# Two transformer blocks on one core: pools held open, row-wise last products and early weight splits around the feed-forward parts

## The chip, the cores and the metric

The kernel runs on one core of one Trainium2 chip. The metric is device time of one execution in microseconds (us), lower is better.

## The reference, cut to what matters

Input `x` is 1024 rows of 1024 floats (float32). Two blocks follow one another. Each has a mixing part and a feed-forward part:

```python
# block 1
h  = rms_norm(x, norm1_g)                     # mixing: forgetting attention, a causal convolution, pooling
x  = x + mix @ w_out                          # w_out 1024 x 1024
h2 = rms_norm(x, norm2_g)
up = causal_depthwise_conv(h2 @ w_up, ffn_dw_w)   # w_up 1024 x 5632, width 3
gate, val = split(up)
x  = x + (silu(gate) * val) @ w_down          # w_down 2816 x 1024
# block 2
h  = rmsnorm(x, pre_mix_w)                    # mixing: differential and neighbourhood attention, two gates
x  = x + rmsnorm(merged @ w_out, post_mix_w)
h  = rmsnorm(x, pre_ffn_w)
f  = (silu(h @ w_gate) * (h @ w_up)) @ w_down # 1024 x 2816 twice, 2816 x 1024
x  = x + rmsnorm(f, post_ffn_w)
```

The factor of the differential attention is `exp(sum(lq1*lk1)) - exp(sum(lq2*lk2)) + 0.2`, from four vectors of 64 (the lambdas).

## The kernel before, in words

Every float32 product is made of three: an operand is split into a rounded part (`hi`, a copy on ScalarE) and a remainder (`lo`, a subtraction on VectorE or GpSimd), and `mm3` (L120) adds hi*hi, hi*lo and lo*hi. So each operand that TensorE reads has a copy and a subtraction ahead of it.

The 1024 rows are 8 blocks of 128. A program is six stages in a row: mixing 1 (`mix1`), its output product (`out1`, L690), feed-forward 1 (`ffn`, L771), mixing 2 (`mix2`, `merge2`), its output product (`out2`, L1297), feed-forward 2 (`ffn`). TensorE does nearly all of the work; the others split, add, normalise and move.

**Output products.** `proj` (L1285) multiplies one row block by 512 columns of the weights: 24 matmuls of 128x512 in all. `out1` adds the result in place to the row block in `rows[i]` and calls `done`, which is `pre_row` (L750): it stores the row to DRAM (`x1D`, on SyncE's queue), normalises it in place, and prepares the operands of the feed-forward. `out2` does the rows 0 to 3 (`second`, L1312) with three `o` buffers, then the columns of rows 4 to 7, opens the pools of the next stage (`early`, L1342), and only then transposes rows 0 to 3. Both are inside `mixing()` (L106), which holds the pools `hT` (the transposed operand, 64 KB a partition), `w` (weights) and `ps` (PSUM: tags tr 2, mm 2, sc 3, pv 1).

**The way up** (`ffn_up`, L789) takes the first product by Strassen's rule in Winograd's form: seven products of half size per channel of 128 columns, with seven transposed operands `T1` to `T7`. `T1` and `T2` are transposed in `pre_row` (`put`, L740); the sums for `T3` to `T7` are formed there (L765 to L768) and transposed after the mixing's pools are closed (`puts`, L902), between the products of channels 0 and 1. A channel's weights come by `weights_a` (L804: two loads of 512 KB and one split) and `weights_b` (L814: sums and three splits); for channels 0 and 1 the loads go out on ScalarE's queue (L897). `lo_of` (L783) sends the subtractions to GpSimd and VectorE in turn, by a counter. There are 22 channels; the result goes to DRAM (`gD`).

**The way down** (`ffn_down`, L966) is a Strassen product again, in groups of 2, 3, 3 and 3 pairs. `load` (L983) brings operands, each is split (L1027 to L1033), and for each of the seven products `DOWN` (L41) four row blocks get 6 or 9 matmuls. `to` (L1003) adds the result to `acc`. In the last group product 7, 4, 3 and 2 follow one another, each for four blocks; `done` (L1044) is called on rows 4 to 7 during product 4 and on rows 0 to 3 during product 2. After the first feed-forward `done` is `stored` (L1381: store to `x2D`, norm in place), after the second it is `final2` (L1411: load `x3D`, norm, add, store). Mixing 2 begins with the transposes of the rows (`to_T`, L170); `lam` (L1065) is called there (L1186).

The order of instructions on each engine is not the program's: the Tile framework orders them by a simulated timeline, with the program's order as priority. Queues run what they got in order. Pools are stacks: one opened after another was closed lies in its memory and waits, tile by tile, for the last use there.

## Time and profile before

| | us |
|---|---|
| median of 3 runs (lowest to highest) | 2841.91 (2841.21 to 2844.3) |
| the profiled execution, its own time | 2845.55 |
| its span, first to last instruction | 2843.8 |
| TensorE busy / VectorE / ScalarE / GpSimd | 2687.9 / 1798.9 / 1200.4 / 891.6 |
| mean granted TensorE clock, as a share of 2.4 GHz | 0.980 |

All durations below come from the one profiled execution. A view by stretches gives the busy time of each engine in a stretch, with the number of instructions behind "x", and the mean granted clock; idle time is the length less the busy time. In a timeline the number in brackets is the idle time of the engine just before the instruction, and what ended it.

### The profile page before, as it was taken

Reading aid. Unit: us, or ns where it says so; the run is one execution under the profiler, and the core shown is the slowest. Engines: PE = TensorE matmul, PEld = TensorE weight load, DVE = VectorE, ACT = ScalarE, POOL = GpSimd, SP = SyncE. Lnnn points to the kernel's source line nnn. Section 1 sums busy time; section 2 is a strip of 40 time slices with the busy share of each in tenths; the row PEclk is TensorE's granted clock in tenths of the full one; section 3 lists DMA queues with packets and bytes.
Section 4 is the critical chain, followed back from the end, with each engine's and each line's share of the span. In section 5 each row is a group of like instructions: output and inputs, shape, how many; then the busy total and the mean of one; then the engine's idle time right before and its main releaser. Section 6 shows DMA issues by size and latency. Waiting matters only on the chain.

```text
span 2843.8 us, 37039 instructions
## 1 busy us (share of the span) xinstructions
PE 2687.9 (95%) x13686; PEld 2258.3 (79%) x13686; DVE 1798.9 (63%) x2748; ACT 1200.4 (42%) x1879; POOL 891.6 (31%) x626
## 2 busy tenths in 40 slices
PE   8999889899999999999999999998997999999997
PEld 7799767678888778788888978887776788887786
DVE  4697574668878799736766443443427555555977
ACT  4344562344544543425545344444323333334333
POOL 3256322123333134611112254422423111211345
PEclk9999999999999999999999999999998999999999
DMA  5445342223332563265554495415412233335722
GB/s 182 122 124 146 115 158 97 82 78 100 107 111 97 207 244 122 93 194 139 155 162 128 126 209 140 133 62 180 157 77 78 82 102 106 111 101 191 260 89 93
DMA packets 317678, 374.01 MB, mean 132 GB/s; under 512 B 42613, under 2 KB 215089, under 8 KB 316985
## 3 DMA queue, kind: packets, MB, share of 16 engines
q1 hardware_dynamic: 309176, 367.45, 41.9%
q10 hardware_dynamic: 8320, 4.19, 0.5%
q8 instruction: 108, 1.77, 0.3%
q14 instruction: 74, 0.60, 0.1%
HBM read 256.49 MB, written 115.08 MB: 131 GB/s over the span
## 4 chain that ended last, share of the span: by engine, by line
PE 69%; DVE 10%; DMA 10%; issue 4%; POOL 3%; ACT 2%; SPq 1%; DVEq 0%; POOLq 0%; ACTq 0%
PE x L118 21%; PE mm L118 20%; PE y L118 11%; PE sc L118 5%; PE z L118 4%; PE pv L118 4%; DVE ac L550 2%; PE tr L359 2%; DVE x L1000 1%; DMA x<-in_w_down_dram 1%; PE tr L1105 1%; DMA x<-gD 1%; DMA mixD<-pvt 1%; DMA wr<-in_w_out_dram 1%; DVE r L1010 1%
## 5 line engine op out<-in xcount | busy, mean ns | idle before, releaser
L139 POOL TENSOR_TENSOR wl<-wr,wh 128x1024 fp32r<-128x1024 f32 x71 | 179.8, 2536 | 359.2 <-ACT wh L138 300.6
L787 POOL TENSOR_TENSOR hl<-x,hl 128x1024 fp32r<-128x1024 f32 x63 | 172.3, 2750 | 278.7 <-ACT hl L1031 197.9
L1031 ACT CAST hl<-x 128x1024 fp32r<-128x1024 f32 x154 | 153.2, 1050 | 221.9 <-PE x L118 123.5
L317 ACT ACTIVATE t<-t,mx 128x640 f32<-128x640 f32 (+3 forms) x192 | 172.9, 901 | 164.6 <-DVE mx L313 156.9
L118 PE MATMUL x<-hl,hl 128*128 128x512 f32 x704 | 214.1, 391 | 3.6 <-DVE hl L787 3.6
L787 POOL TENSOR_TENSOR w<-ws,w 128x1024 fp32r<-128x1024 f32 x44 | 135.4, 3078 | 250.7 <-ACT w L800 250.7
L787 POOL TENSOR_TENSOR w<-wr,w 128x1024 fp32r<-128x1024 f32 (+1 forms) x44 | 85.7, 1947 | 397.7 <-ACT w L800 397.7
L118 PE MATMUL mm<-hA,wh 128*128 128x512 f32 x608 | 197.6, 399 | 4.7 <-ACT gs L1231 4.7
L118 PE MATMUL mm<-hB,wh 128*128 128x512 f32 x608 | 196.7, 397 | 1.0 <-ACT gs L1231 1.0
L365 DVE TENSOR_TENSOR pl<-tr,ph 128x512 fp32r<-128x512 f32 (+2 forms) x160 | 100.5, 634 | 120.0 <-DMA yD<-pvt 42.6
L334 POOL TENSOR_SCALAR t<-t,rs 128x640 f32<-128x640 f32 (+7 forms) x128 | 107.4, 846 | 201.9 <-DVE rs L333 159.8
L877 DVE SCALAR_TENSOR_TENSOR r<-r,fdw,r 128x1024 f32<-128x1024 f32 x88 | 122.2, 1406 | 72.2 <-ACT r L875 72.1
L118 PE MATMUL y<-hl,hl 128*128 128x512 f32 x528 | 161.0, 390 | 5.7 <-DVE hl L787 5.7
L118 PE MATMUL mm<-wh,hB 128*128 128x256 f32 (+1 forms) x752 | 162.2, 305 | 3.0 <-ACT hB L180 3.0
L800 ACT CAST w<-wr 128x1024 fp32r<-128x1024 f32 (+1 forms) x88 | 73.6, 838 | 216.2 <-PE x L118 126.0
L118 PEld LDWEIGHTS x<-hl,hl 128*128 128x128 f32 x704 | 132.8, 189 | 32.3 <-DVE hl L787 4.8
L118 PE MATMUL mm<-wh,hA 128*128 128x256 f32 (+1 forms) x704 | 150.6, 301 | 6.3 <-ACT hA L180 2.1
L787 DVE TENSOR_TENSOR hl<-x,hl 128x1024 fp32r<-128x1024 f32 x91 | 140.7, 1553 | 8.7 <-ACT hl L1031 8.4
L118 PE MATMUL x<-hl 128*128 128x512 f32 x352 | 134.2, 393 | 4.9 <-DVE r L1010 4.7
L118 PEld LDWEIGHTS mm<-hA,wh 128*128 128x128 f32 x608 | 115.5, 192 | 29.2 <-ACT gs L1231 5.3
L843 ACT COPY r<-x 128x512 f32<-128x512 f32 x132 | 76.7, 581 | 145.4 <-PE x L118 87.1
L364 ACT CAST ph<-tr 128x512 fp32r<-128x512 f32 (+2 forms) x160 | 85.2, 542 | 123.7 <-PE tr L359 85.9
(350 smaller groups left out, 7720.5 us busy)
## 6 DMA issues: line engine op xcount, KB each, us to landing
gD<-r SPq DMA_DIRECT2D x154, 256.0 KB
x<-gD SPq DMA_DIRECT2D x154, 256.0 KB
wr<-in_w_up_dram SPq DMA_DIRECT2D x60, 512.0 KB
wr<-in_w_in_dram SPq DMA_DIRECT2D x50, 512.0 KB
x<-in_w_down_dram SPq DMA_DIRECT2D x88, 256.0 KB
wr<-in_w_gate_dram SPq DMA_DIRECT2D x20, 512.0 KB
wr<-in_w_out_dram SPq DMA_DIRECT2D x16, 512.0 KB
QS<-q2D SPq DMA_DIRECT2D x32, 256.0 KB
```

The lines of the kernel that those rows point to most:

```text
L118: self.nc.tensor.matmul(out, lhsT, rhs, start=start, stop=stop, **kw)
L139: g = (lo_engine or nc.gpsimd).tensor_tensor(out=lo, in0=raw[:, :n], in1=hi.bitcast(F32), op=ALU.subtract)
L317: nc.scalar.activation(out=t[:, :nb * P], in_=t[:, :nb * P], func=AF.Exp, scale=-1.0, bias=m, accum_out=s)
L334: nc.gpsimd.tensor_scalar(out=t[:, :nb * P], in0=t[:, :nb * P], scalar1=r, scalar2=1.0, op0=ALU.mult, op1=ALU.mult)
L359: nc.tensor.transpose(tr[:, o * P:(o + 1) * P], ts[qb][:, c:c + P], self.ident)
L364: nc.scalar.copy(out=ph[:, :w], in_=tr[:, :w])
L365: nc.vector.tensor_tensor(out=pl[:, :w], in0=tr[:, :w], in1=ph[:, :w].bitcast(F32), op=ALU.subtract)
L787: return eng.tensor_tensor(out=lo, in0=raw, in1=hi.bitcast(F32), op=ALU.subtract)
L800: nc.scalar.copy(out=hi, in_=raw)
L843: nc.scalar.copy(out=snaps[j], in_=pts[c]["x"])
L877: nc.vector.scalar_tensor_tensor(out=t, in0=src[:, 2 - s:2 - s + S], scalar=self.fdw[:, 2 - s, cc:cc + 1], in1=t, op0=ALU.mult, op1=ALU.add)
L1031: nc.scalar.copy(out=hi, in_=raw)
```

## The change

The pools `hT` and `ps` stay open through the way up: `T4` to `T7` lie in the buffers of the transposed operand, and the way up uses the mixing's PSUM tags. `T5` and `T6` are transposed row by row in `pre_row`; the first weight is loaded and split during the output product (`w_early`). The sums `out1` and `out2` write go to buffers `o` (two in `out1`, one in `out2`), from which rows are stored and normalised; `out2` takes the rows one after another. The first weight loads move from ScalarE's to SyncE's queue (`w_load` issues with `nc.sync`). In the way down, the first splits have a higher priority, the last two products are taken row by row, and the norm's steps by halves; `stored` normalises rows 0 to 3 into other buffers. `lam` is called in mixing 1.

```diff
-        with self.pool("hT", 2) as self.hpool, self.pool("w", 3) as self.wpool, self.pool("ps", 2, PSUM) as self.ps_mix:
+        stack = ExitStack()
+        self.hpool = stack.enter_context(self.pool("hT", 1))
+        self.ps_mix = stack.enter_context(self.pool("ps", 2, PSUM))
+        self.close_mixing = stack.close
+        with self.pool("w", 3) as self.wpool:
             yield
...
+        with self.pool("pe") as pe:
+            gB = self.bcast_row(I["norm2_g"][0], pe)
+            self.w_early(pe.tile([P, D], F32, tag="o", name=self.n("o"), bufs=2))
+            for i in range(NB):
+                o = pe.tile([P, D], F32, tag="o", name=self.n("o"), bufs=2)
+                part(i, 0, w0, o)
+                part(i, 1, w1[6:] if i < 4 else w1, o)
+                done(i, gB, o)
...
-    def pre_row(self, i, rows, keep, gB, jk, T, pool, ps):
+    def pre_row(self, i, rows, gB, src, T, pool, ps):
...
-        self.norm_rows(x, x, jk, gB)
+        self.norm_rows(src, x, x, gB)
...
+        if i == 4:
+            T[6], T[5] = self.T_in("hA", 0), self.T_in("hB", 0)
...
-        self.sums[j] = {6: t2, 5: b11, 7: k0, 4: b21, 3: k1}
+        self.put(T, 6, j, t2, ps)
+        self.put(T, 5, j, b11, ps)
+        self.sums[j] = {7: k0, 4: b21, 3: k1}
...
+    def w_early(self, raw):
+        raw = self.w_load(0, 0, raw.rearrange("p (h x) -> p h x", h=2))
+        self.w_split(0, (1, 2), raw.rearrange("p h x -> p (h x)"), self.nc.vector)
+
+    def w_split(self, c, which, raw, eng=None):
+        w = 512 * len(which)
+        hi, lo = ((self.early_hl.pop().tile([P, 1024], F32R, tag="w", name=self.n("w")) if self.early_hl else
+                   self.fw.tile([P, 1024], F32R, tag="w", name=self.n("w"), bufs=8))[:, :w] for _ in range(2))
+        self.nc.scalar.copy(out=hi, in_=raw)
+        if eng is None:
+            self.lo_of(lo, raw, hi)
+        else:
+            eng.tensor_tensor(out=lo, in0=raw, in1=hi.bitcast(F32), op=ALU.subtract)
...
-            pts[c] = {n: ps.tile([P, 512], F32, tag=n, name=self.n(n)) for n in ("y", "x", "z")}
+            pts[c] = {n: ps.tile([P, 512], F32, tag=t, name=self.n(n), bufs=b)
+                      for n, t, b in (("y", "sc", 3), ("x", "mm", 2), ("z", *(("sc", 3) if c % 2 else ("pv", 1))))}
...
-            weights_a(c, nc.scalar)
+            weights_a(c, nc.vector)
+        T[7], T[4] = self.T_in("hA", 1), self.T_in("hB", 1)
+        T[3] = tuple(fT.tile([P, 4, 512], F32R, tag=f"T3{x}", name=self.n(f"T3{x}")) for x in "hl")
...
+        for c in (0, 1):
+            begin(c)
+            product(c, 1, "x", True)
+            product(c, 2, "z", True)
+            if c == 0:
+                weights_b(0, second=False, eng=nc.vector)
+        snap(0, 1)
+        puts(7)
+        product(0, 6, "x", False)
+        snap(0, 2)
+        product(0, 5, "y", True)
         puts(4)
+        weights_b(0, first=False)
         g11(0)
...
         p7(0)
         v22(0)
+        puts(3)
+        close_sums()
         p4(0)
+        weights_b(1)
         product(1, 6, "x", False)
...
+            def whole(r, h):
+                mss[r, h] = self.sm(1, f"fm{h}", 8)
+                nc.scalar.activation(out=junk[:, :512], in_=acc[r][:, h * 512:(h + 1) * 512], func=AF.Square,
+                                     accum_out=mss[r, h])
+                if h == 0:
+                    nc.gpsimd.tensor_tensor(out=mss[r, 0], in0=mss[r, 0], in1=mss[r, 1], op=ALU.add)
+                    done(r, self.rsqrt(mss[r, 0], 1.0 / D), acc, spare)
...
+            for i in DOWN[:5] if last else DOWN:
+                if gi == 0 and i in (1, 5):
+                    with self.tc.high_priority(offset=100):
+                        hl = operands(i)
+                else:
+                    hl = operands(i)
...
+            if last:
+                h3, h2 = operands(3), operands(2)
+                y2 = [ps.tile([P, 512], F32, tag="b", name=self.n("y")) for _ in range(4)]
+                for i, b in ((3, 0), (3, 1), (2, 0), (3, 2), (2, 1), (3, 3), (2, 2), (2, 3)):
+                    block(i, b, *((h3, y[b]) if i == 3 else (h2, y2[b])))
...
-            with self.pool("lam") as pl:
-                self.lam(pl)
...
-        for i in range(NB):
-            nc.sync.dma_start(out=rows[i][:, :D], in_=xD[i * P:(i + 1) * P, :])
-        with self.pool("pq", 1) as pq:
+        with self.pool("p5", 4) as pp, self.pool("pq", 1) as pq:
+            w0 = []
+            for k in (0, 2, 4, 6):
+                raw = pq.tile([P, D], F32, tag="o" if k % 4 else "gf", name=self.n("o"))
+                w0 += self.pair_in(W, k, 0, raw, [(pp, "woh", 4), (pp, "wol", 4)])
+            for i in range(NB):
+                nc.sync.dma_start(out=rows[i][:, :D], in_=xD[i * P:(i + 1) * P, :])
...
+            half = [first(i) for i in range(4)]
+            for i in range(NB):
+                pts = (self.proj(i, mT, w0), half[i] if i < 4 else first(i))
+                o = pq.tile([P, D], F32, tag="o", name=self.n("o"))
...
+                nc.vector.tensor_tensor(out=o, in0=o, in1=rows[i][:, :D], op=ALU.add)
+                nc.sync.dma_start(out=yD[i * P:(i + 1) * P, :], in_=o)
+                done(i, gB, o)
...
+        o = spare(True) if i < 4 else acc[i]
+        nc.vector.scalar_tensor_tensor(out=o, in0=acc[i], scalar=r, in1=held["g"], op0=ALU.mult, op1=ALU.mult)
```

`pair_in` is a load with a split whose subtraction is VectorE's; `T_in` takes a buffer of the pool `hT` as the pair of one `T`. The last norm (`final2`) does its multiplication, addition and store for the two halves of a row in turn, with all eight rows of `x3D` loaded when the last group begins.

## Rows read from the trace of the kernel before

**Rows 1.** The page, busy time of the engines

```profile
PE 2687.9 (95%) x13686; PEld 2258.3 (79%) x13686; DVE 1798.9 (63%) x2748; ACT 1200.4 (42%) x1879; POOL 891.6 (31%) x626
```

**Rows 2.** Busy time by stretch: from:to, length, PE, PEld, DVE, ACT, POOL, PEclk, DMA, GB/s

```profile
640.00:940.00 300.00, 300.00 (x1310) 244.62 (x1309) 243.09 (x253) 143.86 (x172) 98.38 (x31) 1.00 0.32 103
...
500.00:600.00 100.00, 87.24 (x389) 69.29 (x388) 64.54 (x83) 38.00 (x55) 19.97 (x14) 0.93 0.23 67
955.00:1075.00 120.00, 105.33 (x438) 82.77 (x437) 106.83 (x116) 52.77 (x63) 27.04 (x11) 0.97 0.72 256
1185.00:1230.00 45.00, 38.94 (x243) 35.24 (x242) 31.32 (x36) 21.80 (x34) 23.53 (x19) 0.92 0.52 172
2040.00:2095.00 55.00, 47.94 (x190) 37.77 (x189) 12.42 (x12) 12.72 (x22) 19.72 (x16) 0.91 0.41 152
2130.00:2230.00 100.00, 82.19 (x365) 64.76 (x365) 64.04 (x84) 38.99 (x64) 27.22 (x23) 0.90 0.22 68
2585.00:2695.00 110.00, 101.73 (x434) 81.78 (x433) 89.26 (x102) 45.09 (x57) 24.35 (x10) 0.98 0.74 262
```

**Rows 3.** Prices: chain of waits at 1088.96 (start, us, what); timeline of PE at 2125.99

```profile
1088.96 8.16 PE x L118 x36
...
2125.99 1.04 PE L744 MATMUL tr<-ident,r 128*128 128x128 f32 x8
```

**Rows 4.** Busy time by stretch, transposes of L744 alone (PE, PEld, clock, DMA)

```profile
500.00:600.00 100.00, 12.71 (x84) 10.46 (x84) 0.93 0.23 67
...
2130.00:2230.00 100.00, 16.32 (x96) 12.84 (x96) 0.90 0.22 68
```

**Rows 5.** Timeline of PE at the start of both ways up, the longest stalls

```profile
524.40 0.70 PE L118 MATMUL x<-T1h,w 128*128 128x512 f32 x1 [3.70 <-ACT w L800]
...
543.17 1.16 PE L744 MATMUL tr<-ident,r 128*128 128x128 f32 x8 [2.02 <-DVE T6l L748]
...
2161.71 0.73 PE L118 MATMUL x<-T1h,w 128*128 128x512 f32 x2 [2.14 <-POOL w L787]
```

**Rows 6.** Timelines of VectorE and the chain of waits in the first output product

```profile
518.21 1.28 DVE L188 SCALAR_TENSOR_TENSOR r<-r,rr,wr 128x1024 f32<-128x1024 f32 x1 [3.10 <-DMA x1D<-r]
...
513.93 4.15 DMA x1D<-r
```

**Rows 7.** Timelines of SyncE's and ScalarE's queues and ScalarE at the second way up

```profile
2088.76 68.70 SPq L1326 DMA_DIRECT2D x3D<-r  x8
...
2145.30 0.37 ACTq L808 DMA_DIRECT2D wr<-in_w_gate_dram  x1
...
2154.03 1.04 ACT L800 CAST w<-wr 128x1024 fp32r<-128x1024 f32 x1 [3.63 <-DMA wr<-in_w_gate_dram]
```

**Rows 8.** Timelines of ScalarE and VectorE, a row of the second output product

```profile
2084.15 0.60 ACT L1318 ACTIVATE o<-mm 128x512 f32<-128x512 f32 x1 [6.86 <-PE mm L118]
...
2087.51 1.23 DVE L1325 TENSOR_TENSOR r<-o,r 128x1024 f32<-128x1024 f32 x1
```

**Rows 9.** Timelines of PE and SyncE's queue, from merge2 to out2

```profile
2053.17 0.50 PE L118 MATMUL sc<-wl,hA 128*128 128x512 f32 x1 [2.19 <-POOL wl L139]
...
2070.28 0.83 PE L118 MATMUL mm<-woh,hA 128*128 128x512 f32 x2 [3.65 <-ACT woh L138]
...
2057.64 15.42 SPq L135 DMA_DIRECT2D wr<-in_w_out_dram  x3
```

**Rows 10.** Timeline of VectorE at the end of the first way down

```profile
1205.85 4.32 DVE L188 SCALAR_TENSOR_TENSOR r<-r,rr,x 128x1024 f32<-128x1024 f32 x2 [0.90 <-DMA x2D<-r]
```

**Rows 11.** Timeline of PE at the start of the first way down

```profile
981.37 0.79 PE L118 MATMUL x<-hl,hl 128*128 128x512 f32 x2 [2.12 <-DVE hl L787]
```

**Rows 12.** The end: timeline of PE, and busy time by stretch

```profile
2826.14 0.61 PE L118 MATMUL y<-hl,hl 128*128 128x512 f32 x2
...
2800.00:2827.00 27.00, 26.76 (x119) 21.82 (x117) 23.31 (x23) 10.80 (x15) 15.45 (x11) 1.00 0.22 82
2827.00:2840.00 13.00, 0.00 (x0) 0.00 (x0) 11.02 (x11) 3.95 (x8) 7.84 (x8) 0.69 0.66 245
```

More of the change, by code (lines that the diff above doesn't have):

```diff
@@ L41 @@
 DOWN = (1, 5, 6, 7, 4, 3, 2)
-LATE = (6, 5, 7, 4, 3)
+LATE = (7, 4, 3)
 NX = 26
@@ L717, in out1 @@
             part(i, 1, w1[:6])
-        gB, jk = (self.wpool.tile([P, D], F32, tag="wr", name=self.n("wr"), bufs=2) for _ in range(2))
-        nc.sync.dma_start(out=gB, in_=I["norm2_g"][0].partition_broadcast(P))
-        for i in range(NB):
-            part(i, 0, w0)
-            part(i, 1, w1[6:] if i < 4 else w1)
-            done(i, gB, jk)
+        with self.pool("pe") as pe:
[6 more added lines that the diff above has]
+                done(i, gB, o)
     def right_rows(self, name):
@@ L1029, in ffn_down @@
                     raw = loaded[p][i].rearrange("p a b -> p (a b)")
-                    hi, lo = (fh.tile([P, 1024], F32R, tag="hl", name=self.n("hl"), bufs=12) for _ in range(2))
+                    if last and i == 2:
+                        hi, lo = (fx.tile([P, 1024], F32R, tag="x", name=self.n("hl"), bufs=NX) for _ in range(2))
+                    else:
+                        hi, lo = (fh.tile([P, 1024], F32R, tag="hl", name=self.n("hl"), bufs=12) for _ in range(2))
                     nc.scalar.copy(out=hi, in_=raw)
```

280 lines of the change are left out of this document (128 added, 152 removed).

## The prediction

> **What bounds the kernel.** The page comes first: TensorE is busy 95% of the span, no other engine over 63% [rows 1]. So the next view is busy time by stretch. Inside the first way up TensorE is busy 300.00 of 300 us at full clock [rows 2]; the second looks the same. What TensorE loses, it loses at the seams between stages, and the change touches seams only. For each I count the matmuls and give them the price of an undisturbed run: 8.16 us for 36 matmuls of 128x512 is 0.227 us each, 1.04 us for 8 transposes is 0.13 us each [rows 3]. Length less that sum is the loss, idle time and slow clock together.
>
> - First way up, 500 to 600: 389 instructions, 84 of them transposes [rows 2, 4]. 305 x 0.227 + 84 x 0.13 = 80.1, loss 19.9.
> - Second way up, 2130 to 2230: 269 and 96 [rows 2, 4]: 73.5, loss 26.5.
> - First way down, 955 to 1075: 438 [rows 2]: 99.3, loss 20.7.
> - Second way down, 2585 to 2695: 434 [rows 2]: 98.4, loss 11.6.
> - merge2 to out2, 2040 to 2095: 190 [rows 2]: 43.1, loss 11.9.
> - First way down to mixing 2, 1185 to 1230: matmuls of two lengths, so I take idle time alone, 45 - 38.94 = 6.1 [rows 2]; with the clock of 0.92 it is up to 9.
> - The end: the last matmul ends at 2826.75 [rows 12], the span at 2843.8: 17.
>
> Together some 115 us lie open. Next, timelines at each seam say what ended the stalls.
>
> **The change, part by part.**
>
> *First way up: gain 15.* TensorE waited 3.70 us for the first weight's copy and then stood before transposes whose buffers waited for a subtraction, 2.02 us [rows 5]; the clock was 0.93 in the mean [rows 2]. Afterwards channel 0's first weight is split during `out1`, T5 and T6 of rows 4 to 6 are transposed there, and four products (48 matmuls, 10.9 us) can run as soon as row 7's projection is over. Beside them row 7 takes its chain: add, square, power, scaling, four subtractions, two puts, about 9 us by VectorE's steps (0.6 to 1.3 each, as in [rows 6, 8]). So most of the loss goes; I leave 5 us for channel 1's weights and for T7. Bounds 6 to 18: all of it save the last chain, or only the first wait and its clock.
>
> *Second way up: gain 15.* The same, from a larger loss: TensorE stood 2.14 us for GpSimd's subtraction of a weight [rows 5], and rows 4 to 7 came every 5.45 us (24 matmuls), together with the puts of rows 0 to 3. Now rows 4 to 7 come every 10.9 us. But the new loads of channels 0 and 1 lie in the memory of the weights that row 7 still reads. Before, the third of such loads took from 2145.30 plus about 1 us to 2154.03 [rows 7], nearly 8 us; then copy and subtraction, 2.3. The first two products cover 5.4 us, so I leave a stall of 5, its slow clock and some 6 more. Bounds 5 to 22.
>
> Here the queue matters too. The loads were ScalarE's; now they stand in SyncE's queue among the stores of rows, each of which waits for its row: eight issues spread over 68.70 us, the last at about 2157, while ScalarE's load went out at 2145.30 [rows 7]. A load put behind the last store is up to 12 us late; I count 4 of that in the 11 left. The Trainium skill, "DMA: Bandwidth & Descriptors", section "Issuing engines are not separate DMA queues", says that all issuing engines feed the same 16 DMA engines, so that another issuer saves only the sequencer's time, "usually small relative to the DMA itself". By that sentence the move costs nothing, and the sum would gain 4 more; the row of 68.70 us shows a queue that waits, which the page doesn't speak of.
>
> *Row buffers: cost 6.* In `out1` norms waited for a store to land (3.10 us, the store itself 4.15) because the row was normalised in place [rows 6]; that goes. In its place a buffer `o` is held from the first addition until the store lands, 2.7 + 4.15 = 6.9 us. With two, rows can come every 3.4 us, and rows 0 to 3 want 2.7 (12 matmuls): about 2 us lost. In `out2` there is one `o`: from the square to the end of the addition 2084.15 to 2088.74 [rows 8], plus a store of 4.15: 8.7 us a row, against 5.45 us for rows 0 to 3 and 10.9 for 4 to 7. Two PSUM buffers and the projections that can go ahead cover the most; I take 4. Bounds 0 to 20 (four rows of each product late by the difference and the clock down).
>
> *merge2 to out2: gain 8.* TensorE stood 3.65 us for the weights of the second half, since their loads were queued behind eight row loads (SyncE's queue, 15.42 us for three) [rows 9]. Now these weights load first, four projections instead of three cover them, and the rows follow. The wait of 2.19 us for the first half's last subtraction [rows 9] stays. Bounds 3 to 10.
>
> *First way down to mixing 2: gain 3.* VectorE's norm waited for the store of the row (0.90 us) and ran at twice its cost beside GpSimd (4.32 us for two) [rows 10]. Rows finish one by one now, and out of place. But the buffers of the last operand lie where the low part of the transposed rows goes, so these subtractions wait for the last matmul. Bounds -2 to 6.
>
> *Starts of the ways down: gain 6 of 32.* A subtraction was late by 2.12 us [rows 11], and priority brings that forward; the PSUM of the first blocks comes free earlier. The later stalls there stand beside a VectorE busy 106.83 of 120 us and DMA at 0.72 [rows 2], which the change leaves. Bounds -2 to 15.
>
> *The end: gain 2.* After the last matmul VectorE is busy 11.02 of 13 us, and before that 23.31 of 27 [rows 12]: it is the bound, and its work stays (halves cost a little more). What goes is its idle time and half of the last store. Bounds -4 to 8.
>
> *Lambdas: 0.* Four small loads, a few steps of VectorE and an exponential go from a seam into mixing 1; TensorE covers them there. Bounds -1 to 1.
>
> *The loops: cost 2.* The splits that now name VectorE don't advance the counter of `lo_of`. From channel 2 on, the first way up has each split's subtraction on the other engine: VectorE gets two of 1024 columns (1.2 us each) for one of 1024 and one of 512. It was busy 243.09 of 300 us [rows 2], about 15.6 a channel, and gets 0.6 more. Bounds 0 to 20 (1 us in each of 20 channels).
>
> Sum: 15 + 15 - 6 + 8 + 3 + 6 + 2 + 0 - 2 = 41. The profiled execution took 2845.55 us, 3.64 over the median of the runs; against it 2804.6, against the median 2801.
>
> **The rivals.**
>
> *All seams close.* The upper bounds together (18 + 22 + 10 + 6 + 15 + 8 + 1 = 80) give 2762. For it: VectorE and GpSimd are far from full in the way up's seams (64 of 100 us) [rows 2]. Against: row 7's chain and the loads remain. Chance 0.1.
>
> *The stalls move.* The ways up start late all the same, because channel 0's and 1's loads wait in SyncE's queue or for memory, and the seams of the ways down don't change: 6 + 5 - 6 + 8 + 3 + 2 + 2 - 2 = 18, so 2824. For it: the queue row [rows 7]. Against: the first split no longer hangs on it. Chance 0.2. That priorities change no order (the scheduler may place the splits as before) is in this case.
>
> *Slower: the flipped subtractions.* In the first way up the late split goes to GpSimd beside a VectorE that has the convolution. If a product then waits in each channel, and the clock falls with it, 20 channels pay. It decides from 41 / 20 = 2 us a channel on; at 2.6 us it is 52, a net loss of 11, so 2853. For it: VectorE's 81%. Against: not one wait of TensorE in 300 us [rows 2]. Chance 0.07.
>
> *No change within the bound*, gains and costs cancelling: 0.05.
>
> **How the numbers follow.** Forecast 0.58, with a range of its own from 2781 to 2818; the rivals as above. 2801 is the likeliest. The range of 2780 to 2832 takes in the forecast, the case of moved stalls and a little of the better case. A measurement of this kernel can tell about 0.2% (5.7 us) from no change. Faster by more: 0.58 + 0.1 + 0.2 = 0.88, less 0.01 for the slow edge of moved stalls: 0.87; same 0.05; slower 0.08.
>
> **What would show it.** In the changed profile: the stretch between the last projection and the first full channel has no weight wait over 2 us in the first way up, and one of about 5 in the second; out2's first weight wait is 2 us; idle time at mixing 2's start is some 3 us; the end after the last matmul takes 13 to 16 us; TensorE stays at 300 of 300 in the loops. Wrong if channels lengthen over 19.3 us, if the rows of `out2` are paced by `o`, or if the second way up still loses over 20.

## The result, and the profile after

The changed kernel takes **2809.05 us** (median of four runs, 2807.82 to 2809.56); the kernel before, run beside it, 2841.56 (2839.91 to 2844.3). The ratio is **0.9882, 95% interval 0.987 to 0.9895**: 32.5 us less, where 41 were forecast. The profiled span is 2807.2 us against 2843.8, 36.6 less, and the mean granted clock 0.985 against 0.980.

The page has no other engine near the bound (it answers to [rows 1]):

```profile
PE 2675.4 (95%) x13686; PEld 2253.3 (80%) x13686; DVE 1811.5 (65%) x2772; ACT 1207.4 (43%) x1913; POOL 821.6 (29%) x634
```

TensorE still has 13686 instructions and is busy 12.5 us less: it stands less, and less of its time has a low clock. Where, is read from the starts and ends of the stages in TensorE's timelines of both kernels (us; "way up" begins behind the last matmul of the output product, "way down" at its first matmul):

| stretch | before | after | difference | the prediction's terms for it |
|---|---|---|---|---|
| mixing 1 and first output product | 519.8 | 519.3 | -0.5 | lambdas 0, `o` +2 |
| first way up | 458.2 | 446.3 | -11.9 | -15, loops +2 |
| first way down | 225.2 | 225.8 | +0.7 | starts of both, -6 |
| mixing 2, to the end of merge2 | 845.5 | 848.2 | +2.7 | -3 |
| second output product | 96.5 | 86.3 | -10.3 | -8, `o` +4 |
| second way up | 465.2 | 449.3 | -15.8 | -15 |
| second way down | 216.3 | 218.2 | +1.9 | (above) |
| after the last matmul | 17.05 | 13.7 | -3.4 | -2 |

So four stretches gained about what was forecast or more, the ways down gained nothing, and mixing 2 lost. The next view, busy time by stretch of the changed kernel, answers to [rows 2, 12]; its columns are from:to, length, PE, PEld, DVE, ACT, POOL, PEclk, DMA, GB/s.

```profile
519.20:600.00 80.80, 70.59 (x312) 56.96 (x311) 54.19 (x65) 36.70 (x51) 13.28 (x8) 0.92 0.21 63
600.00:900.00 300.00, 300.00 (x1313) 246.19 (x1312) 244.00 (x250) 143.73 (x171) 59.04 (x32) 1.00 0.33 105
...
965.00:1085.00 120.00, 107.66 (x455) 85.94 (x456) 114.59 (x121) 51.12 (x60) 36.50 (x13) 0.99 0.74 258
1185.00:1205.00 20.00, 15.46 (x87) 13.18 (x86) 12.20 (x15) 9.37 (x18) 8.65 (x12) 0.91 0.62 214
...
1935.00:1950.00 15.00, 13.83 (x47) 10.46 (x48) 5.86 (x9) 5.32 (x9) 3.71 (x3) 0.77 0.66 198
1950.00:1965.00 15.00, 11.89 (x48) 8.76 (x47) 6.46 (x7) 4.81 (x6) 9.99 (x5) 0.95 0.50 154
2040.00:2130.00 90.00, 89.31 (x417) 73.75 (x416) 51.85 (x60) 30.36 (x65) 18.12 (x39) 1.00 0.20 73
2126.00:2206.00 80.00, 68.39 (x308) 53.57 (x308) 49.93 (x67) 32.65 (x50) 16.96 (x11) 0.96 0.27 83
2575.00:2685.00 110.00, 103.38 (x446) 83.27 (x447) 105.97 (x113) 48.66 (x58) 35.52 (x13) 1.00 0.72 256
...
2793.50:2807.20 13.70, 0.01 (x1) 0.00 (x0) 9.72 (x16) 1.45 (x4) 5.21 (x7) 0.60 0.41 154
```

Three things are to be seen. The loops lose nothing (300.00 of 300), and the second output product is full (89.31 of 90). At the start of the first way down VectorE is busy 114.59 of 120 us: a full engine. And a new hole stands at 1935 to 1965, at the start of merge2, with a clock of 0.77. Both kernels wait 3.45 us for the first gate at this place; behind that the kernel before has no wait over 1.35 us, the changed one has 2.80 for a weight's copy and 2.46 for VectorE.

The longest stalls of TensorE in the ways up, from its timeline (they answer to [rows 5]; in brackets the idle time before, and what ended it):

```profile
527.27 1.09 PE L760 MATMUL tr<-ident,t 128*128 128x128 f32 x4 [4.31 <-DVE t L782]
...
574.50 3.01 PE L123 MATMUL y<-hB,w 128*128 128x512 f32 x12 [1.36 <-DVE r L886]
581.82 5.49 PE L123 MATMUL x<-hA,w 128*128 128x512 f32 x12 [4.30 <-ACT r L893]
...
2135.23 0.50 PE L123 MATMUL x<-T1h,w 128*128 128x512 f32 x1 [2.89 <-ACT w L816]
...
2145.51 1.09 PE L760 MATMUL tr<-ident,t 128*128 128x128 f32 x4 [3.83 <-DVE t L782]
```

No wait for a weight is left in the first way up, and one of 2.89 us in the second; the chain of row 7 (`t`, L782) is what TensorE waits for now, and a copy on ScalarE (L893) that the prediction didn't have. In the second way up that chain isn't new: before, TensorE stood 3.45 us for it, longer than the 2.14 us of [rows 5]. And in the first, channel 1's weight stands just beside it: ScalarE's copy of that weight waited for its load and ended at 526.15, 1.1 us before TensorE goes on (TensorE before, then ScalarE of the changed kernel):

```profile
2149.14 0.97 PE L744 MATMUL tr<-ident,t 128*128 128x128 f32 x4 [3.45 <-DVE t L766]
```

```profile
525.11 1.04 ACT L816 CAST w<-wr 128x1024 fp32r<-128x1024 f32 x1 [1.48 <-DMA wr<-in_w_up_dram]
```

Where in the ways up the gain lies, the prediction's own count tells (a matmul 0.227 us, a transpose 0.13; in the first 100 us of each way up the kernel before has 80 transposes, the changed one 64). These are the first 100 and the last 80 us of both, the kernel before, then the changed one:

```profile
519.80:619.80 100.00, 87.97 (x392) 70.00 (x390) 68.80 (x84) 44.38 (x61) 24.45 (x11) 0.93 0.24 74
898.00:978.05 80.05, 76.51 (x326) 61.32 (x324) 57.54 (x60) 36.67 (x45) 17.81 (x6) 0.98 0.41 136
2145.25:2245.25 100.00, 82.19 (x356) 64.60 (x355) 64.27 (x82) 37.68 (x56) 24.74 (x14) 0.90 0.27 82
2530.40:2610.40 80.00, 76.92 (x328) 62.44 (x328) 33.95 (x38) 25.17 (x34) 12.38 (x7) 0.98 0.39 130
```

```profile
519.30:619.30 100.00, 89.80 (x396) 72.72 (x395) 69.66 (x82) 44.81 (x60) 17.01 (x10) 0.93 0.25 77
885.60:965.65 80.05, 78.60 (x343) 63.98 (x342) 61.02 (x64) 38.40 (x47) 12.62 (x7) 1.00 0.36 115
2126.00:2226.00 100.00, 88.39 (x395) 69.96 (x395) 61.27 (x80) 40.10 (x59) 20.66 (x13) 0.97 0.29 90
2495.30:2575.30 80.00, 78.37 (x342) 63.78 (x340) 37.63 (x44) 26.12 (x36) 12.37 (x7) 1.00 0.34 115
```

The loss at the start fell from 18.8 to 16.3 us in the first way up and from 27.0 to 16.5 in the second; at the end it fell from 6.1 to 2.2 and from 5.5 to 2.4. The rest is work that now runs ahead, in the output products: 16 transposes of each way up (2.1 us), and 12 matmuls of channel 0's product with `T2` in the first (2.7 us), of which this is a part:

```profile
503.68 0.63 PE L123 MATMUL z<-T2h,w 128*128 128x512 f32 x2
```

### The profile page after: what moved, and what is told of

The parts are those of the page before. It is cut to its first block, busy times and chain, and to the rows that moved or that the text cites. A ratio compares the mean times of both kernels' runs of the same rounds, so it can differ in the third digit from the quotient of the medians.

```text
span 2807.2 us, 37120 instructions
## 1 busy us (share of the span) xinstructions
PE 2675.4 (95%) x13686; PEld 2253.3 (80%) x13686; DVE 1811.5 (65%) x2772; ACT 1207.4 (43%) x1913; POOL 821.6 (29%) x634
## 4 chain that ended last, share of the span: by engine, by line
PE 74%; DMA 9%; DVE 9%; issue 3%; ACT 2%; POOL 2%; SPq 1%; DVEq 0%; POOLq 0%; ACTq 0%
PE mm L123 23%; PE x L123 21%; PE y L123 12%; PE sc L123 5%; PE z L123 4%; PE pv L123 4%; PE tr L371 2%; DMA x<-in_w_down_dram 2%; DVE ac L563 1%; DVE x L1047 1%; DMA mixD<-pvt 1%; PE tr L1184 1%; DVE r L1057 1%; DVE hl L841 1%; PE tr L760 1%
## 5 line engine op out<-in xcount | busy, mean ns | idle before, releaser
L123 PE MATMUL x<-hA,w 128*128 128x512 f32 x1056 | 257.0, 394 | 4.5 <-ACT r L893 4.3
L123 PE MATMUL mm<-hA,wh 128*128 128x512 f32 x608 | 242.9, 399 | 3.5 <-ACT gs L1308 3.5
L123 PE MATMUL mm<-hA,wl 128*128 128x512 f32 x608 | 240.1, 395 | 0.0
L123 PEld LDWEIGHTS x<-hA,w 128*128 128x128 f32 x1056 | 199.8, 190 | 47.8 <-ACT r L893 5.5
L123 PE MATMUL mm<-wh,hA 128*128 128x256 f32 (+1 forms) x704 | 211.7, 301 | 3.4 <-ACT hA L192 2.8
L123 PE MATMUL mm<-wl,hA 128*128 128x256 f32 (+1 forms) x704 | 210.4, 299 | 0.9 <-DVE wl L144 0.9
L123 PE MATMUL mm<-wh,hB 128*128 128x256 f32 (+1 forms) x704 | 209.7, 298 | 0.2 <-DVE hB L193 0.2
L841 POOL TENSOR_TENSOR w<-wr,w 128x512 fp32r<-128x512 f32 x42 | 54.8, 1304 | 460.1 <-ACT w L816 460.1
L841 DVE TENSOR_TENSOR w<-wr,w 128x1024 fp32r<-128x1024 f32 (+1 forms) x42 | 52.0, 1238 | 179.1 <-ACT w L816 173.7
L816 ACT CAST w<-wr 128x512 fp32r<-128x512 f32 (+1 forms) x86 | 71.6, 833 | 208.5 <-PE x L123 116.5
L927 DVE SCALAR_TENSOR_TENSOR r<-r,fdw,r 128x1024 f32<-128x1024 f32 x88 | 140.0, 1610 | 16.9 <-ACT r L925 16.8
```

Of the source, the lines that this page charges most:

```text
L123: self.nc.tensor.matmul(out, lhsT, rhs, start=start, stop=stop, **kw)
L816: self.nc.scalar.copy(out=hi, in_=raw)
L841: return eng.tensor_tensor(out=lo, in0=raw, in1=hi.bitcast(F32), op=ALU.subtract)
L927: nc.vector.scalar_tensor_tensor(out=t, in0=src[:, 2 - s:2 - s + S], scalar=self.fdw[:, 2 - s, cc:cc + 1], in1=t, op0=ALU.mult, op1=ALU.add)
```

## The experiments

Each stands beside runs of the kernel before on the same chip, so that ratios are compared: the change has 0.9882 (0.987 to 0.9895). An interval is some 4 us wide to either side; smaller effects are read from the stretches of the profiled executions. These have a spread of their own: the changed kernel and those of experiments 1, 2, 3, 5, 6, 7 and 10 wait at the same places of the first way up's start, 10.2 us in all, and yet it takes 443.6 to 443.9 us in five of them (mean granted clock of its first 120 us 0.97) and 445.8 to 446.3 in three, the changed one among them (0.94). There a difference under 2.7 us says nothing.

**1. Row loads of the second output product.** In SyncE's queue of the changed kernel, at merge2's start:

```profile
1909.62 0.43 SPq L1393 DMA_DIRECT2D r<-x2D  x1
...
1912.77 8.62 SPq L1393 DMA_DIRECT2D r<-x2D  x7
```

In the kernel before they went out 140 us later, just ahead of the product that reads them:

```profile
2050.84 3.80 SPq L1302 DMA_DIRECT2D r<-x2D  x8
```

The edit keeps them behind merge2's gate loads:

```diff
-                    nc.sync.dma_start(out=g, in_=self.gD[8 * j + m])
+                    self.mark = nc.sync.dma_start(out=g, in_=self.gD[8 * j + m])
...
-                nc.sync.dma_start(out=rows[i][:, :D], in_=xD[i * P:(i + 1) * P, :])
+                d = nc.sync.dma_start(out=rows[i][:, :D], in_=xD[i * P:(i + 1) * P, :])
+                self.tc.add_manual_dep(d.ins, self.mark.ins.name, NOSYNC, reason="late")
```

> The changed kernel, with the eight loads of x2D rows for the second output product ordered behind the last gate load of merge2 (order alone, no wait added). Theory: merge2 begins 8.5 us late in the changed kernel because these 4 MB now go out at 1909.62 to 1921, ahead of the loads of yD and of the first branch weights (the copy of wh waits 2.80 us, TensorE's clock is 0.77 between 1935 and 1950). Then the stretch from the last matmul of the first way down to the last of merge2 shrinks from 848.2 us by 5 to 9, no weight wait over 1.5 us is left at merge2's start, and the rows land before the second output product needs them, so that this one stays at 86.3: some 2802 in all. Rival: the late start of merge2 comes from its own loads and the stores of the gates in the queue, as in the kernel before; then the stretch shrinks by less than 2 us. A second way to lose: the rows now stand in front of the weights of the second output product as before, which gives back 5 us or more there.

Ratio 0.9837 (0.9823 to 0.985), median 2797.89: faster than the change, the intervals don't touch; the span is 2798.8 us, 8.4 less. The stretch from the first way down to the end of merge2 is 842.4 us (848.2), the output product 86.26. SyncE's queue and the busy time by stretch of this kernel:

```profile
2007.97 1.39 SPq L1393 DMA_DIRECT2D r<-x2D  x3
2012.21 3.66 SPq L1393 DMA_DIRECT2D r<-x2D  x5
```

```profile
1930.00:1945.00 15.00, 13.45 (x58) 10.47 (x57) 5.27 (x8) 6.72 (x11) 3.79 (x2) 1.00 0.66 215
2033.00:2123.00 90.00, 89.31 (x417) 73.77 (x416) 51.45 (x59) 30.82 (x65) 17.60 (x38) 1.00 0.20 71
```

The clock of the stretch is 1.00 instead of 0.77, no weight wait is left there, and the second output product doesn't wait for the rows. The theory holds. Of the 8.4 us, 5.8 stand in this stretch. By the count of TensorE's instructions in mixing 2 the changed kernel is 18.0 us ahead of the kernel before at the 4000th and 9.9 at the 4400th; this one is ahead by 15.2 and 16.2.

**2. The lambdas.** The edit moves the call of `lam` from mixing 1 (L475) back to mixing 2, in a pool with two buffers.

> The changed kernel with the lambdas computed in mixing 2, as in the kernel before, and not in mixing 1. Theory: in mixing 1 they cost 3 us (between instructions 100 and 550 TensorE falls behind the kernel before by 3.1 us, the four loads go out at 48.47 to 49.81 and VectorE waits 3.39 us for them). Then instruction 550 comes 3 us earlier and mixing 2 gets at most 3.5 us longer. Since mixing 1's end stalls on other things, the first output product's end may come 0 to 3 us earlier than 519.3. In all 2806 to 2812. Rival: the 3 us are another order of the same instructions, not the lambdas; then instruction 550 stays where it is, within 0.5 us, and the total too.

Ratio 0.9899 (0.9885 to 0.9913): not faster. TensorE's instruction 550 comes at 93.3 us (94.7 in the change, 93.0 before, so that the change is 1.7 us late there, not 3.1), and by instruction 800 this kernel is behind the change by 0.2. Mixing 1 ends at 519.0. So the theory falls: at instruction 550 the lambdas had 1.4 us, which didn't last. In mixing 2 the stretch got 4.6 us longer, and the trace shows the lambdas there: their loads stopped VectorE 4.34 us ahead of the way down's last addition, and TensorE stood 5.56 us where the change has 0.79 (VectorE, then TensorE):

```profile
1191.98 0.29 DVE L1147 TENSOR_TENSOR lp<-lt 128x128 f32<-128x128 f32 x1 [4.34 <-DMA lt<-in_lambda_k_dram]
```

```profile
1193.68 1.54 PE L189 MATMUL tr<-ident,r 128*128 128x128 f32 x6 [5.56 <-DVE neglam L1153]
```

In the kernel before they ran at 1218.6, and nothing waited for them. So it is the place in the order that costs, not the lambdas.

**3. First splits on both engines.**

```diff
-                    self.lo_of(lo, raw, hi, 2 if gi else 1)
+                    self.lo_of(lo, raw, hi)
```

> The changed kernel, where the first group of both ways down sends every second low subtraction to GpSimd (now all are VectorE's there). Theory: the starts of the ways down gained nothing, because the stalls there (0.8 to 2.1 us each, nine in 120 us) wait for a VectorE that is busy 114.59 of 120 us; the order, which the higher priority changed, isn't what they wait for. Then taking some 14 subtractions of 1.2 us off VectorE lowers its busy time there by 10 to 15 us of 120, and TensorE's busy time in the first 120 us of the first way down rises from 107.66 by 3 to 8: the two ways down get 3 to 12 us shorter together, 2800 to 2806. Rival: VectorE and GpSimd slow each other down (a subtraction of VectorE was seen at 2.4 to 3.4 us instead of 1.2 beside GpSimd), or the stalls are those of loads (DMA share 0.74): then the ways down change by less than 2 us or get longer.

Ratio 0.9959 (0.9946 to 0.9972): 22 us slower than the change by the spans (2829.7), the rival's side by far. The ways down take 235.1 and 222.6 us (225.8 and 218.2), 13.6 us more together; 7.5 stand in mixing 2, where nothing was edited. The timelines of GpSimd, VectorE and TensorE show why:

```profile
967.68 2.38 POOL L841 TENSOR_TENSOR hl<-x,hl 128x1024 fp32r<-128x1024 f32 x1 [15.66 <-ACT hl L1094]
978.24 12.28 POOL L841 TENSOR_TENSOR hl<-x,hl 128x1024 fp32r<-128x1024 f32 x1 [8.16 <-ACT hl L1094]
```

```profile
967.73 2.89 DVE L1047 TENSOR_TENSOR x<-x,x 128x512 f32<-128x512 f32 x1
```

```profile
990.57 3.58 PE L123 MATMUL y<-hl,hl 128*128 128x512 f32 x8 [6.41 <-POOL hl L841]
```

The two engines hold each other up, whichever began first. GpSimd's first subtraction took 2.38 us, and VectorE's of a loaded operand (L1047), begun 0.05 us behind it, took 2.89, where others of its kind took 0.69. GpSimd's second began while VectorE ran one step behind another, and took 12.28 us. The mean of VectorE's subtractions of L1047 rose from 997 to 1235 ns:

```profile
L1047 DVE TENSOR_TENSOR x<-x,x 128x512 f32<-128x512 f32 x36 | 44.1, 1235 | 4.4 <-DMA x<-in_w_down_dram 4.1
```

VectorE's busy time fell only to 107.03 us in 120, and TensorE waited 6.41 us for GpSimd. So VectorE is full there, but handing every second of these subtractions to GpSimd makes it worse. The Trainium skill, "SBUF — State Buffer", section "Who interferes with whom", says that VectorE and GpSimd share a port pair by an exclusive lock, and that a VectorE instruction with two inputs in SBUF contends with GpSimd's reads; these rows agree.

**4. The early split of channel 0's first weight.** Both calls of `w_early` are taken out.

> The changed kernel without the early load and split of channel 0's first weight in both output products: it is loaded and split at the start of the way up, on SyncE's queue like channel 1's. Theory: the early split carries most of the gain of the two ways up (11.9 and 15.9 us), since the first two products can only start on it. Then the first matmul of the first way up comes 4 to 9 us after the last of the output product, that of the second 6 to 14 us, and the sum is 10 to 20 us over 2809: 2819 to 2829. Rival: the gain comes from the pools that stay open, so that the loads find free memory early and T5 and T6 are ready; then the loads hide in the rows' chain and the loss is under 4 us for both.

Ratio 0.9875 (0.9859 to 0.9891), 2808.08 us: no slower than the change. The first matmuls come 3.57 and 4.94 us late, but the ways up as a whole take 448.3 and 450.7 us, only 1.9 and 1.4 more, and mixing 1 with its output product 2.9 less. Most of the 2.9 us are the 12 matmuls of channel 0's product with `T2`, which now run in the way up again. While TensorE waits for the weight, VectorE finishes row 7's chain: the wait of 4.31 us at 527.27 isn't there in this kernel. Two waits stood side by side, and the change removed one. The theory falls.

**5. Where the last operand lies.** `operands(2)` of the last group takes tiles of the ring `hl` instead of the loads' ring `x` (L1090 to L1093 become one line).

> The changed kernel, where the operand of the last product of both ways down lies in the ring of the other split operands, and not in the loads' ring, whose memory the low part of mixing 2's transposed rows takes over. Theory: at mixing 2's start TensorE waits for these low subtractions (1.58 and 1.62 us), which can't run before the last matmul has read that operand; so the first matmul of mixing 2 comes 4 to 5.5 us after the last of the way down, not 6.7. The price: the operand's splits must wait for the last matmul of product 4 (the ring has 12 tiles), which may stop TensorE for 0 to 2 us before product 2 at both ends. Between -3 and +2 in all. Rival: the weights decide, whose loads SyncE's queue lets go only at 1192.64, after the stores of rows; then the first matmul of mixing 2 stays 6 to 7 us behind, and only the cost of the ring is seen.

Ratio 0.9902 (0.9887 to 0.9916). The first matmul of mixing 2 comes 7.7 us after the last of the way down (6.75 in the change), and TensorE still waits 1.19 and 1.17 us for the same low subtractions. So the memory of that operand is some 0.4 us of each of these waits (1.58 and 1.62 in the change). The end after the last matmul grew to 16.9 us (below).

**6. The stores of rows on another queue.**

```diff
-        nc.sync.dma_start(out=x2D[i * P:(i + 1) * P, :], in_=acc[i])
+        nc.scalar.dma_start(out=x2D[i * P:(i + 1) * P, :], in_=acc[i])
```

> The changed kernel, with the eight stores of x2D at the end of the first way down issued on ScalarE's queue instead of SyncE's. Theory of the queue: these stores hold SyncE's queue for 20.30 us until 1192.64, and mixing 2's first weights wait behind them; on the other queue the weights go out before 1189 and are split before the last matmul, and the first matmul of mixing 2 comes 1 to 3 us earlier than 6.7 us after the last of the way down. Rival: the low part of the transposed rows decides, which lies in the memory of the last operand: then it comes at 6 to 7 us all the same, or later, since ScalarE's copies now stand behind stores that wait for their row.

Ratio 0.989 (0.9874 to 0.9907). The weights went out 17 us earlier, but their copy ran only at 1200.08, behind ScalarE's squares and copies of the last rows (SyncE's queue, then ScalarE):

```profile
1175.90 1.67 SPq L140 DMA_DIRECT2D wr<-in_w_in_dram  x2
```

```profile
1200.08 1.05 ACT L143 CAST wh<-wr 128x1024 fp32r<-128x1024 f32 x1
```

Mixing 2's first matmul came 9.8 us after the way down's last, later than in the change. Neither of the two causes that I had for this seam is enough by itself. In the changed kernel two chains end side by side. One is that of the last row, in VectorE's timeline:

```profile
1191.51 0.69 DVE L1057 TENSOR_TENSOR r<-y,r 128x512 f32<-128x512 f32 x1 [0.55 <-PE y L123]
1192.99 1.28 DVE L1451 SCALAR_TENSOR_TENSOR x<-r,rr,x 128x1024 f32<-128x1024 f32 x1 [0.79 <-POOL rr L163]
1194.19 0.68 DVE L193 TENSOR_TENSOR hB<-tr,hA 128x512 fp32r<-128x512 f32 x1
1195.27 1.28 DVE L1451 SCALAR_TENSOR_TENSOR x<-r,rr,x 128x1024 f32<-128x1024 f32 x1 [0.39 <-POOL rr L163]
```

From the last addition (1191.51) over square, power and scaling to the last row's transposes (1197.21) are 5.7 us. The other is the first weight's, in ScalarE's timeline:

```profile
1196.97 1.05 ACT L143 CAST wh<-wr 128x1024 fp32r<-128x1024 f32 x1 [0.76 <-DMA wr<-in_w_in_dram]
```

This copy waited for its load and ended at 1198.02; the first matmul ran at 1198.22. Experiment 5 leaves both chains, and experiment 6 takes the load's wait away but puts the copy further back. That the two chains are the limit is argued from these rows; no run took both away.

**7. The last two products in turn.** The block behind `if last:` (L1127 to L1131) is taken out and the loop runs over all of `DOWN`; the operand of product 2 lies in the ring as in 5.

> The changed kernel, with the last two products of both ways down one after the other, as in the kernel before (all four row blocks of product 3, then all of product 2; the last operand in the ring as well, the steps by halves kept). Theory: row by row is what shortened the end after the last matmul from 17.05 to 13.7 us, since rows 0 to 2 are through before the last block; in turn it is 16 to 18 again, +2 to +4 us. Rival: the halves and the early loads of x3D did it: then it stays at 13 to 14.5. At mixing 2's start I expect the same 6 to 7 us, within 2.

Ratio 0.9909 (0.989 to 0.9928). After the last matmul this kernel takes 18.7 us, the kernel of experiment 5 takes 17.0, the change 13.7 (busy time by stretch, this kernel, then that of experiment 5):

```profile
2795.70:2814.40 18.70, 0.03 (x1) 0.00 (x0) 13.16 (x21) 2.89 (x8) 7.20 (x12) 0.62 0.37 142
```

```profile
2795.00:2812.00 17.00, 0.09 (x1) 0.00 (x0) 13.05 (x21) 4.34 (x12) 6.26 (x12) 0.59 0.42 158
```

Against the change the end is 5.0 us longer, and VectorE has 13.16 us of work left behind the last matmul instead of 9.72. But this kernel differs from the change in two things. Experiment 5, with the order by rows in the program and only the last operand in the ring, loses 3.2 us of the five; the order on top of it is worth 1.8. So order and place of the operand carry the end together, and the order by itself is not shown to give the theory's 2 to 4. Halves and early loads alone give nothing: the kernel before has 17.05.

**8. T5 and T6 late, no early split.** On top of 4, the `put`s of T6 and T5 go from `pre_row` to the way up (`puts(6)`, `puts(5)` ahead of product 6), with four buffers for `t2`. A part of T5 (row block 3) is then read after product 1's copy has taken its buffer, so that this part of the computation is changed.

> The changed kernel without the early split, and with T5 and T6 transposed in the way up, after the first products, as in the kernel before; what stays of the change at the way up are the pools held open, the single weight ring and the new order of rows. The kernel without the early split alone showed that the first matmul of the ways up then comes 3.57 and 4.94 us late, and that all but 2 and 1.4 us of it comes back behind it, as VectorE finishes row 7's chain meanwhile. Theory: T5 and T6 in the rows are what carries the gain of the ways up: their 64 transposes (8 us at 0.13) and 16 subtractions leave a seam where VectorE is late. Then the stretches from the last output matmul to the first of the way down are 448.3 and 450.7 plus 4 to 10 us each, 2815 to 2830 in all. Rival: the open pools (memory free for the first loads and operands) carry it; then both stretches grow by less than 3 us, which the transposes alone cost, and the total stays under 2813.

Ratio 0.9911 (0.9896 to 0.9925). The ways up take 451.7 and 452.6 us, 3.4 and 1.9 more than in 4, and the output products 1.4 and 1.8 less: some 2 and 0 net. Net of that it is the rival's side in the stretches, though the first one alone is 0.4 over its 3 us. Even without early split and early T5 and T6 the ways up are 6.5 and 12.6 us shorter than before. The total is over the 2813 that it allowed, but for another reason: mixing 2 with merge2 took 853.7 us here and 847.8 in 4.

**9. One buffer for the copies.** An edit of one line that the prediction had passed over:

```diff
-        snaps = {1: t1, 2: t2, 3: t3, (0, 2): R[2][:, :512], (NF - 1, 2): s1}
+        snaps = {1: t1, 2: t2, 3: t3}
```

A row block of T4 is then read after channel 0's copy has taken its buffer, which changes that part of the computation.

> The changed kernel without the extra buffers for copies of the running sum: channel 0's second copy and the last channel's second copy go to the common buffer again, as in the kernel before (one line). Theory: part of the gain of the ways up lies at their ends, which the prediction did not count. Before, TensorE waited 2.73 and 2.35 us for ScalarE's copy of the last channel (11 us before the way down), and the clock of the last 78 and 80 us was 0.98; in the changed kernel these waits are gone. Undone, the last 65 to 70 us of each way up get 2.5 to 4 us longer, some 6 us in all, 2813 to 2817; the starts, where channel 0's copy waits for a read that is done early, stay within 1 us. Rival: the wait at the end was that of the operands' transposes or of PSUM, whose tags changed too: then the ends stay within 1 us of the changed kernel's.

Ratio 0.9876 (0.9862 to 0.9889). At the ends the waits of the kernel before are back to the hundredth, 2.73 and 2.35 us. TensorE's timeline at the end of the first way up:

```profile
950.69 3.02 PE L123 MATMUL x<-hA,w 128*128 128x512 f32 x12 [2.73 <-ACT r L893]
```

So this part of the theory holds. But the first way up got 5.3 us shorter as a whole (441.1), 2.6 against the kernels with the same waits as the change and the higher clock. At its start the waits of 1.36 and 4.30 us had gone, with 0.88 and 0.68 in their place, and the clock of its first 120 us was 0.99; the theory had that start unchanged. ScalarE's timelines tell: here the convolution's first scaling of channel 0 runs at 559.24, in the changed kernel both scalings only at 574.48 (first this kernel, then the changed one):

```profile
559.24 1.18 ACT L925 ACTIVATE r<-r,fdw 128x1024 f32<-128x1024 f32 x1
```

```profile
574.48 2.20 ACT L925 ACTIVATE r<-r,fdw 128x1024 f32<-128x1024 f32 x2 [0.91 <-DVE r L886]
```

The change puts channel 0's copy into `R[2]`, which is also the convolution's buffer `b_`: the scaling that writes there waits until the copy is read (the addition at 573.76), and the next copies stand behind it on ScalarE.

**10. Without the priority.** `operands(i)` is called without `high_priority`.

> The changed kernel without the higher priority of the first splits in the ways down. Theory: VectorE is what the starts of the ways down wait for (114.59 us busy of 120, and the kernel that gave half of it to GpSimd got slower), so the order of the splits changes little: the two ways down, from their first matmul on, stay within 1.5 us of 225.82 and 218.20, and the first matmul comes 0 to 2 us later after the last of the way up, since the first copies stand further back. In all 2809 to 2813. Rival: the priority brings the first splits forward as forecast, and without it the stretch up to the first 60 us of the ways down is 3 to 8 us longer each, 2815 or more.

Ratio 0.9868 (0.9854 to 0.9881). The ways down take 225.76 and 218.37 us (225.82 and 218.20), with the same waits. The priority does nothing; VectorE is full.

**11. First loads on ScalarE's queue**, on the kernel of experiment 1:

```diff
-        self.nc.sync.dma_start(out=t.rearrange("p h (k m) -> p (h k) m", k=4),
+        (self.nc.scalar if c < 2 and keep else self.nc.sync).dma_start(out=t.rearrange("p h (k m) -> p (h k) m", k=4),
```

> The kernel with the late row loads, in which the three loads of channels 0 and 1 that start the ways up (the first one is early and stays) are issued on ScalarE's queue, as in the kernel before. Theory of the queue: on SyncE's queue they stand between the stores of rows, whose five issues hold it for 38.34 us, until 2119.48; the second way up then waits 2.96 us for channel 1's operand and its clock falls. On ScalarE's queue they go out earlier, by the time the weights of the last rows leave their memory, and the second way up's start gets 2 to 5 us shorter: 2793 to 2796. Rival, after the Trainium skill's page on DMA bandwidth and descriptors: another issuer saves only its own time; the loads wait for memory that the last projection reads, and go out at the same time within 1 us; then nothing changes, 2796 to 2800, or the copies of ScalarE stand behind the waiting issues and it gets 1 to 3 us longer.

Ratio 0.9848 (0.9834 to 0.9863), against 0.9837 without this edit: nothing gained. The first load goes out at 2121.78 on ScalarE's queue, 0.19 us before the last projection's end at 2121.97; on SyncE's queue, in the kernel of experiment 1, it went out 0.16 us before that end at 2119.64 (this kernel's row first, then that one's):

```profile
2121.78 0.38 ACTq L802 DMA_DIRECT2D wr<-in_w_gate_dram  x1
```

```profile
2119.48 0.38 SPq L802 DMA_DIRECT2D wr<-in_w_gate_dram  x1
```

The loads waited for the last projection's reads, whoever issued them. The rival holds.

**12. The copy in another buffer**, on the kernel of experiment 1: `(0, 2): R[2][:, :512]` becomes `(0, 2): s1`. A row block of the sum for T3 still lies there, so this part of the computation is changed; `s2`, whose sum has been transposed by then, would be free, and was not run.

> The kernel with the late row loads, in which channel 0's second copy goes to the buffer s1 (free since product 7's transposes) and not to the buffer of the convolution (one word changed). Theory: in the changed kernel the convolution of channel 0 can't begin before that copy is read (its first two scalings run together at 574.48, just behind the addition of 573.76), and the following channel's copies stand behind it on ScalarE: TensorE waits 1.36 and 4.30 us at 55 and 62 us of the first way up. In the kernel with one buffer the scaling of the second half runs at 559.24 and these two waits are 0.88 and 0.68. So with the copy moved the first way up, 443.80 us with the late rows, gets 3 to 7 us shorter, the second (no convolution) stays within 2 of 450.12, and both ends keep their short waits (0.68 and 0.73): 2791 to 2796 in all. Rival: the 4.30 us went with the kernel with one buffer because its whole order differs (the last channel's part too); then the wait stays and the total is 2796 to 2800.

Ratio 0.9813 (0.9798 to 0.9827), 2792.74 us; the interval just touches that of experiment 1. The first way up takes 438.9 us (443.6 in the kernel of experiment 1, 445.8 in that of 11), the second 449.3. In TensorE's timeline both waits have gone, one of 0.96 is left; the theory holds:

```profile
583.24 0.74 PE L123 MATMUL y<-hB,w 128*128 128x512 f32 x2 [0.96 <-ACT w L816]
```

## Why the prediction was right or wrong

The sum of 41 met 36.6 in the spans; the sign, the bound and four of the seams were right, and 2809 lies in the range. Several causes were wrong all the same, and that the sum came so near is in part luck: a cost of 6 that did not come and some 7 us gained at the ends of the ways up, which no term had, stand against 6 that the ways down did not give and 6 that the row loads took back.

- **First way up, gain 15:** 12.4 with the half microsecond of the output product. The size was near by luck; the cause was not. I left a loss of 5 us at the start; by the same count it is 16.3, only 2.5 less than before. "So most of the loss goes" because the first split and T5 and T6 come early: they are worth 0 (experiment 4) and some 2 us (8). Of the gain, 4.8 us are work that the output product took in, and 3.9 stand at the end, where the last channel's own copy buffer, which I didn't count, takes a wait of 2.73 us away (9). Channel 0's adds 1.36 and 4.30 at the start and costs 4.7 in all (12). The step that failed is that "four products (48 matmuls, 10.9 us) can run" beside row 7's chain: channel 0's product with `T2` ran inside the output product, only the 12 matmuls of its product with `T1` stand behind it, and channel 1's two had no weight before 526.15. So TensorE stops 3.6 us behind the last projection and waits 4.31 us for the chain (527.27), which takes some 8 us, near the forecast. In the kernel of experiment 11, where channel 1's products stand ahead of row 7's transposes, TensorE waits 3.55 us for that weight instead:

```profile
526.91 0.79 PE L123 MATMUL x<-T1h,w 128*128 128x512 f32 x1 [3.55 <-ACT w L816]
```

  What the open pools, the PSUM tags and the order of rows each gave, in this way up and the second, no run tells apart, and it stays open.
- **Second way up, gain 15:** 15.8, of which 10.5 at the start, 3.1 at the end and 2.1 of moved work. The stall forecast as 5 us is 2.89 for the weight, with 3.83 for row 7's chain behind it, for which the kernel before waited 3.45; the loss left at the start is 16.5 us, where I had 11. **The queue**, of which I counted 4 us, costs nothing (11). The rule of the Trainium skill that I weighed against it ("DMA: Bandwidth & Descriptors", section "Issuing engines are not separate DMA queues") gave the right answer. My row of 68.70 us showed a queue that is held, but not that a load behind it could have gone earlier.
- **Row buffers, cost 6:** 0. The rows of `out2` are not paced by the one `o`: TensorE is busy 89.31 of 90 us.
- **merge2 to out2, gain 8:** 10.3 there, and given back. The step that failed is "and the rows follow": I had the row loads go behind the weights, at 2050. With nothing to hold them they went to the start of merge2 instead, and cost 6 net (848.2 against 842.4 us, experiment 1), 8.1 by the count of instructions at that place. The wait of 2.19 us that was to stay is 0.21.
- **First way down to mixing 2, gain 3:** 1.5 in idle time, 6.06 us before (2.96 and 3.10) and 4.55 after, where I had some 3. The wait for the stored row and the doubled scaling of [rows 10] are gone; the last row's chain and the first weight's, which end within 1 us of each other, take their place. My cause for the loss, the memory of the last operand, is some 0.4 us of each of two waits (5).
- **Starts of the ways down, gain 6:** none, 0.7 and 1.9 longer; the second is 215.5 us in the kernel of experiment 1, which has no edit there, so the 1.9 says little. I wrote that the later stalls stand beside a full VectorE; the early ones did too. Priority changes no wait (10), and GpSimd can't take the work (3).
- **The end, gain 2:** 3.4, by the order of rows and the place of the last operand together (5, 7), while I had counted on idle time and the last store. I called VectorE's work there fixed; with these two, part of it is done before the last matmul.
- **Lambdas 0, loops -2:** the lambdas about 0 in mixing 1 (2); called where experiment 2 has them they cost some 4. The loops lost nothing, so the rival of the flipped subtractions has no ground; that of the moved stalls came true only for the ways down.

## What to carry to other kernels

A wait that is removed is worth what the next one leaves: see which chain ends just behind it before counting its length. When an edit sets a load free of what held it, ask where in the order it will go, since a prefetch may land on a stage that was full; keeping eight loads back was worth 8.4 us of span, where the whole change was worth 36.6. Read each new buffer for what else lives in it: of two entries in one line, one took waits of 2.73 and 2.35 us away, the other cost 4.7 us.

## What the runs showed that I had not expected

- A subtraction of 128x1024 on GpSimd that took 2.38 us where it began first took 12.28 where VectorE's were under way, and VectorE's of 128x512 took 2.89 instead of 0.69; giving GpSimd half of the first splits made the ways down 13.6 us longer.
- Loads issued on either queue went out within 0.03 us of each other, measured against the end of the matmuls that read their memory.
- Small edits change the order of the whole program: mixing 2 with merge2 took 848 to 856 us in the ten kernels with the early row loads (the changed one and those of experiments 2 to 10), most of them with no edit there.
